# A new order and a new choice of engines for the same 4,836 steps of a one-core layer kernel

## Chip, core and metric

The kernel runs on one core of a Trainium2 chip. Its time is the device time of one execution in microseconds, the median of several runs. A core has five engines with a queue each, worked off in order: TensorE (PE; its weight loads are listed as PEld), VectorE (DVE), ScalarE (ACT), GpSimd (POOL), and SyncE (SP), which here issues the transfers. An instruction at the head of a queue that waits for another engine holds up everything behind it.

## What is computed

One layer of a decoder trunk on 512 tokens of width 1024, in float32: a normalised and modulated input goes into one projection whose columns feed a recurrent head group (convolution, RG-LRU scan) and an attention group (compressed, selected and windowed keys), then an output projection, a residual, and an MLP with a squared ReLU.

```python
for l in range(DEPTH):
    mod = jax.nn.silu(c) @ ada_w[l] + ada_b[l]
    sh1, sc1, g1, sh2, sc2, g2 = jnp.split(mod, 6, axis=-1)
    h = modulate(rms_norm(x, pre_norm_mix[l]), sh1, sc1)
    y = hybrid_mixer(h, w_in[l], ...)     # z = h @ w_in; rnn and att from its columns; concat @ w_out
    x = x + (1.0 + g1[:, None, :]) * rms_norm(y, post_norm_mix[l])
    h = modulate(rms_norm(x, pre_norm_mlp[l]), sh2, sc2)
    y = jnp.square(jax.nn.relu(h @ w_ff1[l])) @ w_ff2[l]
    x = x + (1.0 + g2[:, None, :]) * rms_norm(y, post_norm_mlp[l])
```

## The kernel before

Every float32 matmul is done in three: a weight tile `raw_w` is split into `hi_w` (a rounded copy, often on ScalarE) and `lo_w` (the difference, on VectorE or GpSimd), the activations likewise into `h` and `h2l` or `lo`, and TensorE adds the three products (`mm3`, L948). The sequence is four blocks of 128 tokens.

The program is written as streams, generators that record steps instead of issuing them (`Clocks.record`, L295). The order of work along the time axis is: the opening up to about 20 us (streams XL, WM, XN, SU, TR, MW), the projections of `h` (PR, with AW and the compressed keys; until about 160 us), the recurrent group's vector work (VW: scan over `r`, gates `g0` to `g3`, whose projection result in the PSUM bank `f` is copied to `r` by ScalarE), attention scores (AS: matmul `s<-K,Q`; `p<-s,tab` on VectorE; the exponential `p<-p,mx` on ScalarE; the scaling `p<-p,den` on any of three engines), attention values (AV: transposes `tp<-ident,p`, their copies `pt<-tp`, matmul `pv<-pt,V`), the output projection (CO, FA: `f<-hi_o,h`; weights `raw_o`), the residual and second norm (RS), its transposes (TH: `h`, `h2l`), the up projection (UF for its first two slices, `pv<-h,hi_f`; then UP, `f<-h,hi_f`), the first down pass (DA, with sums of weight blocks `raw_A..` and of activations `fs`), and the second down pass (DN, from 525 us) with the last norm and the stores. Beside all of them run the modulation sums (AD: `ar<-ar,silb`, `accT`), the loads (WL) and the splits of weights (WS).

Two tables fix what happens on the chip. `PLACE` (L69) has, for each stream, one letter for each step that can run on more than one engine: a (ScalarE), d (VectorE), p (GpSimd); `Clocks.put` (L305) reads it. `PLAN` (L90) lists all 4,836 steps, two characters each, and `Clocks.flush` issues them in that order. So the order in each engine's queue is the order of its steps in `PLAN`, the transfers on SyncE's queue among them:

```python
text = "".join(PLAN)
for a, b in zip(text[::2], text[1::2]):
    (way,) = self.nodes[ALPHA.index(a) * len(ALPHA) + ALPHA.index(b)].ways
    way[2]()
...
mine = PLACE.get(self.name, "")[k:k + 1] if PLACE is not None else "adp"
ways = [w for w in ways if w[0][0] in (usual if mine in ("", ".") else mine)]
```

Matmuls are at L396, transposes at L400, ScalarE's operations at L407, VectorE's and GpSimd's at L441, stores at L483.

Of the kernel before, what the change touches and what calls it, by code (L numbers as in the profile page):

```python
# [15 lines left out]
P = 128  # L16
S = 512
D = 1024
# [77 lines left out]
    '2d372E2K2~2G3S2c2j2g2e2f382b2l2i333V3T2k39352r2h2n342/2m2q363W2*2p3X2%2o2-3*3!3U2,3x3#2<2]3c3Y2?2=3y3C3Z'
    '3I3$2:3a2{2@583d2^3O3F3D3z3b3%3e3h3&3J3n3+3P3(3L3i3o3,3R3)3t4#3k3/4H3?3u4%3:3q4F3{3@45463w3A473G3M484M2.'
    '3|3f4O494C3l3r4A3<4N4B3-4g3=4G4$4h4i4k4l4m4j4Q4^4&4n4P4+4o4,4-4]GY4(4.2+2>4~4S5L504)2;514*3]5K4/2[4_3~4{'
    '4d2_3^5Y3E413K3Q52425D3B5X5M4|4}59533H3j445E5h5A5B5C435F5H5G3N5g5J3p3v5O3g3m5I5N5S3;5$3[5P3s4b7%5T3.5R3>'
    '4a3_3}4J5Q5#5Z5U5V5a5b5i5j5k4I5-5W5l5m5d5n5o5p5q5,5r4X5s7&4V5t5u4K5e627)6;4c6-5v4L5w6<6.6/5x6=5y615z5f6d'  # L100
    '5!5%6>6e4W6f7>6N674U6_6M5c6:7(68696@6A7?6V6B6{6?6C4e4R6D5_6E5&4Z4T6g6F4Y6G6H6I6U5(5)6[6J6|7+6K4f6q6}6L7|'
    '6h6O5*6p6P6i5+6]6^816Q6~6R6j6y5.5/6S6x6T6W5:726k5{716l6X6m6n5;5<7a6Y5=5>6a5?7b5@5[6Z5]73706o7c5^5}5|6r5~'
    '6c607C636s7B646t7R6u656v6w6b667N746z6!7S7D6#6$6%8L7z757T6&7@7!766(7[7o7]7}6)7~80777*7#788279836*847A7s85'
    '7t7p6+7q86877M88897r8A8B7w7u8V8W7vGW8Z8C8D8X7x7E8b7^8K8d937F8Y947,8E7-977_7.GZ957G997H7y7I9&7/8e4E7J8j9('
    '7K8k9)7L9+7O8h8F9,7P8f6,8G8O8i9E8P8QGa987Q7U9A9F7V8R9I7W9K7X9J9G7Y8M8S7Z8g7$7d8T7:7e8c9:7fG@9H8^8_9L8{9;'
# [1704 lines left out]
```

## Time and profile before

| | |
|---|---|
| median of 3 runs | 627.62 us (626.68 to 628.64) |
| the profiled execution's own time | 627.82 us |
| its span, first to last instruction | 626.0 us |
| PE, DVE, ACT, POOL busy | 95%, 86%, 55%, 33% of the span |
| PE instructions, weight loads not counted | 3060 |
| mean granted clock of TensorE | 0.991 of full speed |

The profile is of one execution. PE counts as busy from the start of a matmul to its modelled end, so that back-to-back matmuls overlap a little and short gaps between them don't show.

### The profile page before, as it was taken

What the parts mean: (1) busy time and instruction counts of PE and PEld (TensorE: products, weight loads), DVE (VectorE), ACT (ScalarE), POOL (GpSimd) and SP (SyncE); (2) the same over time, 40 slices, a digit from 0 to 9 for tenths busy, and PEclk for the clock granted to TensorE, in tenths of its full rate; (3) what the DMA queues carried; (4) which work ended last, traced back from release to release, by engine and by line L of the source; (5) the groups of instructions that cost most, each with busy time, mean ns of one, the idle gap of its engine ahead of it and who ended that gap; (6) DMA issues with size and microseconds to landing.
All of it is one profiled execution on the core that took longest, in us unless ns stands there. A gap on an engine that the chain in (4) does not pass through costs nothing.

```text
span 626.0 us, 9043 instructions
## 1 busy us (share of the span) xinstructions
PE 596.3 (95%) x3060; PEld 497.9 (80%) x3060; DVE 539.2 (86%) x1072; ACT 346.1 (55%) x696; POOL 209.1 (33%) x209
## 2 busy tenths in 40 slices
PE   7999999998999999989999999999999999999992
PEld 6888788966777898869887888888887888878881
DVE  5986988979999988988888968787688789999897
ACT  6654525698999999687251220322322247465563
POOL 5001301652663175453204547641351231000113
PEclk9999999999999999999999999999999999999997
DMA  8968895430503302015664334254544426756613
GB/s 351 416 250 318 320 299 191 131 136 1 202 2 129 141 2 102 1 35 176 229 222 168 115 133 137 101 169 157 180 135 147 155 69 204 238 179 202 198 56 134
DMA packets 29430, 102.15 MB, mean 163 GB/s; under 512 B 3268, under 2 KB 3524, under 8 KB 29384
## 3 DMA queue, kind: packets, MB, share of 16 engines
q1 hardware_dynamic: 29240, 101.50, 46.4%
q8 instruction: 24, 0.39, 0.3%
q14 instruction: 22, 0.18, 0.1%
q10 hardware_dynamic: 144, 0.07, 0.0%
HBM read 99.47 MB, written 2.10 MB: 162 GB/s over the span
## 4 chain that ended last, share of the span: by engine, by line
PE 73%; DVE 11%; DMA 6%; ACT 5%; issue 3%; DVEq 0%; SPq 0%; ACTq 0%
PE f L396 36%; PE s L396 14%; PE pv L396 13%; PE tp L396 7%; DMA ar<-in_ada_t 4%; PE tp L400 4%; DVE r L441 3%; ACT p L407 2%; DVE fT L441 2%; ACT r L407 2%; DVE ar L441 1%; DMA raw_A11l<-in_wd 1%; DMA raw_A10l<-in_wd 1%; DVE p L441 1%; DMA r<-in_x 1%
## 5 line engine op out<-in xcount | busy, mean ns | idle before, releaser
L396 PE MATMUL f<-h,hi_f 128*128 128x512 f32 x224 | 87.7, 392 | 0.0
L396 PE MATMUL f<-h,lo_f 128*128 128x512 f32 x224 | 87.2, 389 | 0.0
L396 PE MATMUL f<-h2l,hi_f 128*128 128x512 f32 x224 | 87.2, 389 | 0.0
L407 ACT ACTIVATE fT<-f 128x512 f32<-128x512 f32 x30 | 17.8, 594 | 71.2 <-PE f L396 71.2
L396 PEld LDWEIGHTS f<-h,hi_f 128*128 128x128 f32 x224 | 42.1, 188 | 8.8 <-issue 0.2
L396 PEld LDWEIGHTS f<-h2l,hi_f 128*128 128x128 f32 x224 | 42.0, 188 | 8.6
L396 PEld LDWEIGHTS f<-h,lo_f 128*128 128x128 f32 x224 | 42.0, 188 | 8.5
L396 PE MATMUL f<-hi_o,h 128*128 128x512 f32 x128 | 47.7, 414 | 0.0
L407 ACT ACTIVATE p<-p,mx 128x32 f32<-128x32 f32 (+4 forms) x96 | 45.1, 472 | 3.8 <-DVE mx L441 3.6
L441 DVE TENSOR_TENSOR lo_f<-raw_f,hi_f 128x1024 fp32r<-128x1024 f32 x29 | 40.1, 1383 | 6.9 <-ACT hi_f L407 6.6
L400 PE MATMUL tp<-ident,p 128*128 128x128 f32 x192 | 41.6, 273 | 1.9 <-DVE pt L441 0.9
L396 PE MATMUL pv<-pt,V 128*128 128x256 f32 x160 | 42.2, 316 | 1.1 <-ACT pt L407 0.7
L441 POOL TENSOR_SCALAR p<-p,den 128x32 f32<-128x32 f32 (+4 forms) x43 | 35.7, 863 | 18.5 <-DVE den L441 15.5
L396 PE MATMUL s<-K,Q 128*128 128x288 f32 (+4 forms) x128 | 38.4, 336 | 0.5 <-DVE Q L441 0.3
L441 DVE TENSOR_TENSOR pt<-tp,pt 128x512 fp32r<-128x512 f32 (+1 forms) x56 | 33.6, 609 | 3.3 <-ACT pt L407 1.9
L407 ACT ACTIVATE hi_f<-raw_f 128x1024 fp32r<-128x1024 f32 x24 | 24.9, 1056 | 18.7 <-PE f L396 13.0
L396 PEld LDWEIGHTS pv<-pt,V 128*128 128x128 f32 x160 | 27.8, 189 | 6.1 <-DVE pt L441 2.1
L396 PE MATMUL s<-r,fs 128*128 128x512 f32 x96 | 32.5, 389 | 0.0
L396 PE MATMUL pv<-r,fs 128*128 128x512 f32 x96 | 31.8, 391 | 0.4 <-DVE r L441 0.4
L400 PEld LDWEIGHTS tp<-ident,p 128*128 128x128 f32 x192 | 25.0, 140 | 7.8 <-issue 1.8
L396 PE MATMUL tp<-r,fs 128*128 128x512 f32 x96 | 30.6, 389 | 0.0
L441 DVE CUSTOM_DVE_ANT_0 ar<-ar,silb 128x1024 f32<-128x1024 f32 x16 | 21.6, 1352 | 6.4 <-DMA ar<-in_ada_t 6.4
(732 smaller groups left out, 1817.0 us busy)
## 6 DMA issues: line engine op xcount, KB each, us to landing
raw_f<-in_wf SPq DMA_DIRECT2D x32, 512.0 KB, 3.5
p<-in_ada_a SPq DMA_DIRECT2D x16, 512.0 KB, 8.0
ar<-in_ada_t SPq DMA_DIRECT2D x16, 512.0 KB, 4.4
ar<-in_ada_r SPq DMA_DIRECT2D x16, 512.0 KB, 4.0
r<-in_x SPq DMA_DIRECT2D x8, 512.0 KB, 4.6
raw_c<-in_wc SPq DMA_DIRECT2D x8, 512.0 KB, 5.2
raw_o<-in_wo SPq DMA_DIRECT2D x8, 512.0 KB, 6.4
raw_a<-in_wa SPq DMA_DIRECT2D x8, 384.0 KB, 7.5
```

Source lines behind the costliest of these rows:

```text
L396: lambda: self.nc.tensor.matmul(out, lhs, rhs, start=start, stop=stop))
L400: self.issue("pe", 0.109, [out], [src], lambda: self.nc.tensor.transpose(out, src, ident))
L407: return "act", cost, lambda: self.nc.scalar.activation(out, src, func, scale=scale, bias=bias, **kw), func
L441: return eng, cost, lambda: fn(out, *args, **kw), None
```

## The change

Nothing but `PLACE` and `PLAN` differs: the same 4,836 steps with the same operands. 259 steps get another engine (69 each in WS and DA, 59 in AS, 12 in AV, 10 in AW, 9 in TH, 8 in DN, 7 in UP, 6 in VW, 5 in FA, 4 in XN, 1 outside any stream). TensorE has 2,922 steps before and after and 207 transfers are issued; ScalarE goes from 568 to 573 steps, VectorE stays at 938, GpSimd from 201 to 196. TensorE's order changes from its second instruction until the first down pass, most steps by fewer than 60 places; the second down pass keeps its order on TensorE. On SyncE's queue the first 33 loads are the same; after them neighbours are exchanged, by 1 to 12 places.

```diff
 PLACE = {
-    'AS': 'papaaaadapadapdppadpddpdpapddapadppdpppapapppdaadddddaapdpdaadpdpapadddppaaappppdappppppapppapap'
-        'appapadppdppaadd',
-    'AV': 'dadaadddddaddddaaddadaaaaaaaaadaaaadaaaadaaaadaaaadaaaad',
-    'AW': 'adadaaddpppddpdp',
+    'AS': 'paaaappddaaadapddppdppappddpdaaadpadpppadppppppddppdaaaddadappadppappppaapaaapadpddpppppddpdapap'
+        'pppapadapddpaaaa',
+    'AV': 'aaaaddadddaadddadddddaaaaaaaaaaadaaaaaaadaaaaaaadadaaaad',
+    'AW': 'aaaaaaaadpdpddpd',
...
-    'FA': 'dddppdpdpddp',
+    'FA': 'pppppppddddp',
     'RS': 'ppadddddadda',
-    'TH': 'daddaadpddddaadddddddappddpddadd',
+    'TH': 'ddddaapdadddaadddddpaadpddddaadd',
...
-    'VW': 'pppdddpddppdppppppp',
+    'VW': 'dpddppppdppdppppppd',
...
-    'XN': 'aaaaaadaaaaa',
+    'XN': 'aaaddddaaapa',
 }
 PLAN = (
-    '000O0P020Q0106400R0S0T0U0V0M074p4q084r0a0W0y040b4sGX4t090c030&0d0X0A554u0C4v054w0e4x0(0-4y0Y0H0N4z4!0D4:'
...
+    'q_p{p|p}qJq5qIq6q7q3q8p;q9qAqfqBqCqDq4qEqFqGqLqhqMqgqNqOqPqQqXqiqRqSqTqUqVqYqWqZqcqdqKqeqjqlqmqaqnqqqoqr'
...
```

Decoded, this is the order of four stretches (step's output<-input; a stretch of one engine's queue):

```
ScalarE, projections' end
  before: sigmoid r | exp r x4 | sqrt r x2 | Q<-f x2 | r<-f (g0) | sqrt r x2
  after:  sigmoid r | exp r | r<-f (g0) | exp r x3 | sqrt r x3 | Q<-f x2 | sqrt r
VectorE, start of the MLP
  before: h2l_1 | h2l_0 | h2l_2 | h | r<-f | h | lo_f0 | r<-r,h x2 | h2l_5 | h2l_4
  after:  h2l_0 | h2l_1 | h2l_3 | r<-f | lo_f0 | h2l_4 | h | r<-r,h x2 | h2l_6 | h2l_5
          (h2l_3 comes from GpSimd, h2l_2 goes to it; one h of ScalarE's nine transposed copies ahead of
           hi_f0 goes to VectorE, one h of VectorE to ScalarE, behind hi_f0)
GpSimd, opening of the projections
  before: lo_x0 | r<-r,vecs | r<-r,vecs
  after:  lo_x0 (both r<-r,vecs are on VectorE)
GpSimd, tail
  before: ar<-ar,fT | ar<-ar,fT | fT15<-ar,g2row1
  after:  ar<-ar,fT | fT15<-ar,g2row1 (the second ar<-ar,fT is on VectorE, stat<-stat ahead of where it was)
```

## Rows read from the trace of the kernel before

**Rows 1.** The page, part 1: the span, and of each engine its busy time, share of the span and instructions.

```profile
span 626.0 us, 9043 instructions
...
PE 596.3 (95%) x3060; PEld 497.9 (80%) x3060; DVE 539.2 (86%) x1072; ACT 346.1 (55%) x696; POOL 209.1 (33%) x209
```

**Rows 2.** The view of windows, by stage (from:to and length in us, then the busy us of each engine in it with its instructions, the granted clock of TensorE as a part of full speed, the DMA share and rate).

```profile
0.00:100.00 100.00, 92.21 (x524) 79.07 (x525) 81.96 (x163) 52.28 (x84) 15.71 (x28) 1.00 0.85 319
100.00:145.00 45.00, 44.66 (x257) 36.14 (x258) 38.57 (x126) 37.47 (x105) 20.11 (x18) 1.00 0.38 129
145.00:200.00 55.00, 49.09 (x261) 39.03 (x259) 53.31 (x157) 52.28 (x135) 30.14 (x31) 1.00 0.21 78
200.00:262.00 62.00, 62.00 (x402) 54.34 (x401) 56.68 (x166) 54.55 (x134) 28.14 (x38) 1.00 0.22 77
262.00:300.00 38.00, 35.22 (x234) 31.83 (x233) 33.23 (x53) 28.34 (x48) 16.02 (x21) 0.96 0.32 103
...
526.00:626.00 100.00, 87.51 (x384) 71.66 (x383) 91.89 (x129) 53.37 (x82) 14.31 (x9) 0.96 0.51 170
```

**Rows 3.** The view of waits of TensorE over the whole span: which matmul (its output) waited for which engine's instruction, us in total, number of waits, the longest.

```profile
PE f L396 <- ACT r L407: 2.9, 2, 1.9
PE pv L396 <- DVE lo_f L441: 1.4, 1, 1.4
PE pv L396 <- ACT hi_f L407: 1.1, 1, 1.1
PE tp L400 <- DVE pt L441: 0.9, 1, 0.9
PE s L396 <- POOL r L441: 0.8, 1, 0.8
PE f L396 <- DVE Q L441: 0.8, 1, 0.8
PE pv L396 <- ACT pt L407: 0.7, 1, 0.7
PE s L396 <- DMA raw_c<-in_wc: 0.7, 1, 0.7
...
PE f L396 <- DVE fs L441: 0.5, 1, 0.5
```

**Rows 4.** The timeline of ScalarE from 139 to 149 us: start, duration, what it does (xN: N of a kind in a row), and in brackets the idle time before it with its releaser.

```profile
140.53 2.57 ACT L407 ACTIVATE r<-r,sp 128x512 f32<-128x512 f32 x4
143.11 1.28 ACT L407 ACT_TABLE_LOAD   x1
...
145.72 1.20 ACT L407 ACTIVATE Q<-f 64x512 fp32r<-64x512 f32 x2 [0.15 <-PE f L396]
146.94 0.60 ACT L407 ACTIVATE r<-f 128x512 f32<-128x512 f32 x1
```

**Rows 5.** The timeline of TensorE at the same place, the same columns.

```profile
145.28 0.40 PE L396 MATMUL f<-h,lo_q 128*128 128x512 f32 x1
147.59 0.50 PE L396 MATMUL f<-h,hi_g 128*128 128x512 f32 x1 [1.91 <-ACT r L407]
```

**Rows 6.** The timeline of VectorE from 270 to 284 us, where the MLP begins.

```profile
273.69 1.64 DVE L441 TENSOR_TENSOR h2l<-h,h 128x256 fp32r<-128x256 f32 x3
...
276.36 0.53 DVE L441 TENSOR_SCALAR h<-tp,a,s 128x256 f32<-128x256 f32 x1
276.81 1.21 DVE L441 TENSOR_TENSOR lo_f<-raw_f,hi_f 128x1024 fp32r<-128x1024 f32 x1
```

**Rows 7.** The view of windows around the first MLP matmuls, the columns of rows 2.

```profile
276.00:280.10 4.10, 2.35 (x15) 1.91 (x16) 3.89 (x7) 3.57 (x7) 2.26 (x3) 1.00 0.25 78
280.10:283.50 3.40, 3.40 (x17) 3.40 (x18) 2.83 (x4) 3.28 (x4) 0.48 (x1) 0.50 0.15 60
```

**Rows 8.** The timeline of VectorE and then of GpSimd from 67.5 to 74.5 us.

```profile
68.41 3.32 DVE L441 CUSTOM_DVE_ANT_0 ar<-ar,silb 128x1024 f32<-128x1024 f32 x1 [0.60 <-DMA ar<-in_ada_t]
...
68.27 2.37 POOL L441 TENSOR_TENSOR lo_x<-raw_x,hi_x 128x1024 fp32r<-128x1024 f32 x1 [17.91 <-ACT hi_x L407]
```

**Rows 9.** The timelines of the tail, 609.5 to 626 us: VectorE, then GpSimd.

```profile
611.04 1.32 DVE L441 TENSOR_TENSOR stat<-stat 128x1 f32<-128x1 f32 x2
...
610.71 1.57 POOL L441 TENSOR_TENSOR ar<-ar,fT 128x512 f32<-128x512 f32 x1 [0.83 <-ACT fT L407]
613.51 1.55 POOL L441 TENSOR_TENSOR ar<-ar,fT 128x512 f32<-128x512 f32 x1 [1.24 <-ACT fT L407]
```

**Rows 10.** Groups of instructions between 145 and 262 us, one shape each (line, engine, operation, output<-input, shapes and count, then busy us and mean ns of one, then idle time before): GpSimd, ScalarE, VectorE.

```profile
L441 POOL TENSOR_SCALAR p<-p,den 128x384 f32<-128x384 f32 x3 | 3.9, 1316 | 1.4 <-DVE den L441 1.4
...
L407 ACT ACTIVATE p<-p,den 128x384 f32<-128x384 f32 x7 | 4.1, 606 | 0.3 <-ACT p L407 0.3
...
L441 DVE SCALAR_TENSOR_TENSOR accT<-ar,sil,accT 128x512 f32<-128x512 f32 x8 | 6.0, 745 | 0.0
...
L441 DVE TENSOR_TENSOR_SCAN r<-p,r 128x512 f32<-128x512 f32 x4 | 5.9, 1476 | 0.0
L441 DVE SCALAR_TENSOR_TENSOR lo_o<-raw_o,vecs,hi_o 128x512 fp32r<-128x512 f32 x8 | 5.8, 740 | 0.0
...
L441 DVE TENSOR_TENSOR lo_o<-raw_o,hi_o 128x1024 fp32r<-128x1024 f32 x3 | 3.8, 1260 | 0.0
...
L441 DVE TENSOR_SCALAR p<-p,den 128x384 f32<-128x384 f32 x6 | 2.7, 476 | 0.0
```

More of the change, by code (lines that the diff above doesn't have):

```diff
@@ L96 @@
[L96 to L105, printed above, removed]
@@ new lines @@
+    '0o1E0p1k0q15141F171v1G0[19161B180r1A1D1H1l0s1w1I0t1M0u1J0v1N0w1=0x1Q1W0$1V1m1U1K1n1o1>1b1p1x1q0<1r1c1@1T'
+    '1]1L1R1s1Z1S1?2L1[1t1Y1^1_1{1a1|1X1e552Q1u1z1}1i1h2M1%201f1d1g0]2x541$211+1y2X1#1;1~221&2&1-2O2N1,2s232P'
+    '1<2y1!2R28052E2t2z2S2T292V1*1:2F2Y2U1)1(272K2W2Z1.262v302u2(2a2D2w1/2g56252}2)242!312f2#322A2|332B2$2C2H'
+    '2G372m2~2c2%2I2i383V2J2l3c2b2e3S392r2o352/2?2,343T2{2d2j2*2h362p2:2k3y2-2@2=2n3W2^3U3d3D2<2]3!3x2q3e2.3*'
+    '3J3C3#3I3z3X4G3+3Y3O3Z3A3P3F3a3,3L3$3%4#3R3(3k3b4%3i3h4H3&3q2>3G3n3)3t3/3?573{3M463o3u3:453@3|482+4M2;47'
@@ new lines @@
+    '3f4N3w3l4B3<4O3r3-4C4$4g494h4i4A2_4j4]3E4^4k2[4&4l4Q4m5L4n4R4(4F3=4o3^4T4+424,4P4-3K414.GX3]4~434S4)4*3B'
+    '5K4/50514_4{3H4|5X5Y4}3Q523N535D44595h5E3j5M3~5A5B5N3g5S5F3p3v5C5O5H5g5G5P5J3;3m5Q5Z5$5a5I3[5R3s5b5V3.5i'
+    '5j5#3>5k5l5m3_5T5n5-4J5o5p4d5q5r5W3}4I5U5s5t5d5u5v5,7%5w5x4U6d7&4b6e4L5e626;7(6-7)5c6.4K5y5z6<5!6=6/6:4c'
+    '67616>4V5%68694W6@6_7>6N5&4X6f0N5f6{4a4Y5(6[6A6M6B5)5*5+5.4Z6g6V6C6D6?587?6E6]6|6U6h6}6F6^6G6H4f5_6q6I6i'
+    '6~7+6J7|725/6j6p736k5:6l6K5{5;6y5<6L5=765>5|6x6O745?6P6Q6m716R6S6T6W6X5@7a6Y5[6n756Z5]7b5^6a6o5}6r6c7c5~'
@@ new lines @@
+    '6sGY60777063646t7R6u6v6b7C656w667o7S6z6!6#6$7z6%7p7B78797@7[7A7D6&7T7!7]7}6(7~7N807q7r6)7E7w7s7M8283848V'
+    '858W7t7u8X8ZGW7v8b866*877x7,7^8d887F817G8e897#7H7-8A936+7I7.7J8j7_8B8C8f8h7K8k4e948D7L7O977P954E8K7Q7/8E'
+    '8Y8F8G7U8c8O999EGZGa7V8P7y8Q9F7W7*8R9&987X8S7Y8g7Z9KG@7d8T7:967e7f9A7$7g7h7;8i8^8_8L7i9G8a9I8{7<9(7j8U8|'
+    '7=8}8l6,8~9:9L9;8u909H8m8v9+8w8s8r8x917k929J9B8y9<8t8z8q8!8#7l8$9=8%8&9C8(8H8n8)G]8*9D8+9V9W9)8,9M8o8-7m'
+    '8.9,9lAUAO8/9N8p8:8I9r9R8;8<9U8=8>9m9X8?9sAP9S9Y8J9Z8@9n9t9o9aG[AQ8[9b9OAVAS9v9Q7{9c9w9uAR9xAp9p9P9yAW9z'
@@ new lines @@
+    '9!9#9*8]9$8M9q9%AX9d9eA59f7nAv9gAqAE9h9-9TAFB.Aw8N9.G^9/9>AGA69?ArA79iG_9@B/9[AtAH9]9j9^AIAxA8CbCcATCdAJ'
+    'A.C99_A/9{CiA9CjAYAuAKA>CAALCkAMCpA?AyCqAACrAZCBABC#AaA<AcC$C%A:Ab9|A;A@9}9~C+A=AdAeBDHPBEAzA0BLAgCNC,AN'
+    'AfA!A#ACAhADA(AiAjBFAsC-BJCOA$BHA[C/A%A)BtBKA1A&BIC:BMA2BGB1B5A*C;A3BuBRAkA]B2BPC<9kBNAlC=B6B3A+BvA,A^B4'
+    'B,A~BwA-A|A_B7C1A}AmHQB-BhA4BiA{HRHbC_C2C>B:B9C3B0CWHSCPCXCHB8C4BjBACIBkCQBnBBCJCVAoCRBlCUBCCLAnCKBmBoBp'
+    'CMBxCSBcC{C|CZC~CTBqByC@BrD0C[C]DVBdD1BzC^B#D2ChD3CaB!D4BsDWD6CYD7DPD8CeD9DQB$CuDAB%DBDCB(CmDDDXDEDFCoDG'
@@ new lines @@
+    'DHCvDICfDJCwDKB&CnDRDSDLCzB)DTDMDUC)DYB*CtDZDOC!B+DaDeDbDND$BeClC*DuFhDcDdC&DhD@D[CxD]DiD^C?BODjD_B;DvD%'
+    'D{DkD!C(D&D|DwDyD}BSBfDlBgDmD#D+DnCsCyBQB<DoDpDxDqBTD)DzCgD~BUC}DrD*DsE6D,E0E1D(E7DtBaE2D-BVBZBbD.EsC.BX'
+    'EtBYEuEvBWEwD=B@FjB|D5ExECB[E*B]E3B^E+EAD<B}EDE,B=DfE[B_E]E^B~E_E{EBB>FlE4E8EEEaEbB{E|EgFAFnEeEhEQFBE9Ei'
+    'E5EGEFEcFCC0D?FIEjD>FJHEFKFdEdFeD/F%HFC5E-FfE=EfE.EHEIE/FgE;C6EkC7D:C8F|E>ElB?EJD;FLErEWFkEKE?EmELEpFRF&'
+    'CCEREXFMEqESEMFPFSG1ENFoCDEYH>HNETFNEOFTF,EZEnEPEUEoF~G,F}F<CEG0FiF4F5F=HKF6EVF7FmF-EyG-F.CGEzE}G3E!CFE#'
@@ new lines @@
+    'E$F:E~HLG4E%L)F0F1F>GUF_F2GxHeGrF8GsL*G.F3E&FpHJE<F9FtGVG6FuFqH?L(E)FvGyE(FrDgFwGvG/FsF(GtG:F{FOFzF!H4FD'
+    'H5FxH@E@F#H[FGGzF$G;G2G8H6F)FyHAFHHBE:H]G5FQH8HGH^HCHHFUH_H{F*H#HDG9FVG7F@HpGuH$FWHOGAF[HqF+FZGNH%GBHIFa'
+    'GCHrGOHtIUH9H:IFGPH7GHGIFbGJGKFcGDIGGLH&GQH|H}GRHsGMGlGSGmHuGnGTGoGhFYGiG!GjH;H(GpGbGcGkFXFEH<GdGeGqH~H='
+    'FFI0GfGwHZF?GgIYHcG<I1IVH)G{G=IZF]IHF;HdIWH*G|IaIJG>HMI?F/HaJSL&IXI!I#I)HYG#I*IKI&I@G?G$H0I+G}JTG)H1GEI$'
+    'JUG~JVI(HfH2I[IIH3JWG*G(JHHgJLJXI%HTJ.GFG%HhHjHiJ/I,JMHkG+HvG&HlGGH/JNHmI6HwJOHnHUHxJPHVI7JII-HoI2H+JBHy'
@@ new lines @@
+    'J:HXHzJ;JQI.J<I;H!JRI9I3I4I5IAMlHWILJCH-I8IMIBICIQI/J=IDJFJ?J@JDJ>JJJ[H.IRIPJ]H,JzJ^J_MnIbJtINKOKPISIEIO'
+    'MvKQJuIfIcKHJEIgKqI>J!JvKrITI:IdI=MwI<JxKIJKIoIeIhIpIqIrIiMmK8IsIjIkIuJwIvIwItKsJyKtIxMoKuIlKvIyKwJ#KJMs'
+    'MtI|K9IzKxI]JGI^MuI_I}I~J$J7KCJ0KAI{KDJ1J3J%J4J5KGJ8KKKEKiJ2KjKFJ6JYKmJ9KkKyJhJiJ&KzKnJAJ-JZK/KoJaKBJbK:'
+    'JjJcInJkJ*JnK[K=JlLSLTK;J+KpK]JoJmLULhJpK<J,LCLDKlImJdK^K0JqJ{LELiJrK1J|LjJeLGJsLpLHK_J}LqLtLKKWKXLFJfKY'
+    'K{KLK2J~KMLIK3LuLJK4K|J(K5JgKcK}KNK6KZLrLvL0LwKaL1K7KdM0L2LsLxKeKbKRL!M1KSL3LyL#KTK>KfL$J)M4KgM5K!K#KUK&'
@@ new lines @@
+    'L%K$M2M6KhK(K%McM3MdM7K)LVK+LzLWK,K*LXK-LYMeMgLbLZK.LcL7KVLdM8LeK?LaMhL8M:LfL+K@M9MAL,MiL/L9MkMEL4L:MfLg'
+    'L;L-L.L<M>LAL=L5LBL?L@L^F^LkM?L>L_L{L|L[LnM@L]M;L}MQL6MRLLK~OrL~LMLoMSMTLNMDM<MFMUMVMYMZOpMWNCNDNHLOMXMj'
+    'MHNEMaOqM*MLM+M,NIM-MbNGMCM$M.OtMOM%LPM[MIMGNsMPM/LQOuOxN2MyNJN3NtMzLRN6N4NuM]OvNKN7NwN8OsM^N5MpMBO@M&Oy'
+    'MqOwM=N^NxMxM_MrN!M{M~MMNyN0N_M|N}N{O[N9NFN~M}NANaN1NLOMNzONNTNBOzNbNeNfNgO0O]NvNcNdNhNoM(O^NMNiM)NUNSNk'
+    'NlNRNmNjNpNVNWNPO_O!NnO{NNNXNQNqN#O#N-LlN$OQMNO|NYNrN|N.N%NZO}N/O~N:NON=P0N>N;ORLmN&N?N(N@N)N<PVN[O2OSPi'
@@ new lines @@
+    'OON*M!PjN]MJO6P1O3O7O8OTO4O5OCOGO9OHOPODOAP4PWOUOIOEPXOFOBPkO1OdOJPYP2N,MKOeOKPlOVPZOWP5OfOZOgOLOhOiPmOl'
+    'OaOjPnO*OmOYOkPoObOnN+P3PpPqOcO+OoO:P6O,O-PaO.O;PrO$O%PbO/O&O<O=PcO>PdOXO)PsPBPtO?PFPCPDPGPuPEPHPIPPPLPJ'
+    'PeO(PMPfP7PQPKPgPNPRPSPhPOP(P,PTP)P8P*Q2P9PvQ3PUQ4P-M#P+Q5P.P:PAP;P<PwP/P=P>PxPyP?QPQQQ6PzQRP@P[P]QSP^QT'
+    'Q7P!P_QVQ8P{QUQ9QAP|P#QXQBQWQCQDP}QYQEP~Q0P$QZQ1P%Q[Q]Q^QaP&QdQFQ_QxQ{QbQeQnQcQfQgQIQoQ|QhQpR8QJQiQqR9RA'
+    'QrQGRBQkQyQHQsRCQjRDQtQKQ)Q*QuQ+Q,QzQ-Q!Q#Q.Q$REQvQ%QLQ&Q}QlQ(Q=QmQ~Q>QwRPQ?QMR0Q@QNQ/RRRQR1RSRFQ;R2RTRU'
@@ new lines @@
+    'RvQ:RGRwRxR3RyRHRzRJR!R#R4R$R%R&RIR(R5R)R*RVR6Q<R7R+SWR,RWR-R.R/R_R{R|R}QOR~RKS0RXS1S2S3SERYSFSGSHSISJSK'
+    'SLSMRLSNRZSOSPSQSRSSSTSURaSVSZRMSaSbScRNSdSeSfSgShSiROUGSjSkSlSmSnSXSoRlSpUHSqSrRbRcSsRdStUDSuSYReSvSwSx'
+    'SyRkRfRmUERnSzRoUJS!RgS#RqS$S%S&RhS(RpS)S*S+S,RrS-UIS.R:R;RsR<R=RtS/UNS:R>S;RiS<S=S4R?RjS5S6S7S>S?S8R@S@'
+    'RuS[S]S^S9R[S_S{S|S}SAR]S~T0T1R^SBT2T3T4SCT5T6T7SDT8T9UFTATBTCTDTETFU2TGTHUOTITJTKU3TLTMTNTOU1TPU5TQTRUP'
+    'U4TSUQTTTUTVTWTXTYUKTZTaURU6USUgTbULUhTcTdTeTfUMUUUiUjUkVEUlUaUmVFUnU7TgThVGVPTiUbUoTjUqTkU8UrUcTlTmTnUV'
```

143 lines of the change are left out of this document (52 added, 91 removed).

## Prediction

> **What bounds the kernel now.** I read the page's first part first. TensorE is busy 95% of the span, VectorE 86%, ScalarE 55%, GpSimd 33% [rows 1]. The same 2,922 TensorE steps run after the change, at the same sizes, so the time can only come out of TensorE's idle time, out of its clock, or out of the ends. TensorE's idle time is 626.0 - 596.3 = 29.7 us. The view of windows says where it lies [rows 2]: 7.8 us in the first 100 us (4.7 us of it is the wait for the first load), 0.3 from 100 to 145, 5.9 from 145 to 200, none from 200 to 262, 2.8 from 262 to 300, and 12.5 after 526, nearly all of it the tail behind the last matmul. Between 300 and 526 there is next to nothing to be had, whatever the order is. Then I read the view of waits, which gives these gaps their names [rows 3]. So the stakes are 3.1 us of the opening, 5.9 us of the attention stage, 2.8 us at the start of the MLP, 0.5 us in the second down pass and a tail that can hardly shrink: about 12.5 us, 2% of the time. A change that moves 259 steps and shuffles thousands can bring a per cent at most, and each wait that it makes new costs as much as one that it removes.
>
> The attention stage needs a second look. From 145 to 200 us VectorE is busy 53.3 of 55 us and ScalarE 52.3, while TensorE has 49.1 [rows 2]. TensorE waits there because two other engines are nearly full; if one wait goes, TensorE comes sooner to the next step that they have not done yet. So a gain in this stage is limited by what the two are relieved of, not by the sum of the named waits.
>
> **Part by part.** Durations are from the profiled execution: 627.82 us, of which 1.8 lie outside its span and stay; it stands 0.2 above the median of 627.62.
>
> *The gate projection.* TensorE stands still from 145.7 to 147.59 us, because the next gate block needs a PSUM bank that ScalarE has not copied out [rows 5]. ScalarE's copy (`r<-f`, 0.60) runs at 146.94, queued behind four exponentials (2.57), a table load (1.28), two square roots and two Q copies (1.20) [rows 4]. The new order puts it behind the first exponential, ahead of the other three. The Q copies at 145.72 stand between square roots and bring no table load of their own [rows 4], so a copy costs its 0.6 there too. But TensorE's order changes with it: the matmuls between the end of g0 and the first of g2 shrink from about 5.6 to 2.0 us (counted at 0.23 us for 512 columns, the distance of back-to-back starts), and in that time ScalarE has to finish an exponential (0.7) and the copy (0.6). That fits with some 0.5 us to spare. The wait of 1.9 goes; bounds -1.9 and 0. The second such wait (2.9 in two, so 1.0) keeps its cover of 1.3 us and stays [rows 3].
>
> *Attention's own waits.* Of the waits for `pt` and Q, three get more TensorE work ahead of them by my count of the tables: the transposes behind `pt` (0.9; cover 0.85 before, 1.2 after), the `pv` matmul behind ScalarE's `pt`, which moves to VectorE (0.7; 0.06 to 1.2), and the score matmul behind Q (0.3; 0.6 to 2.4) [rows 3]. A copy takes 0.6 to 0.7 us, so the last two go and the first halves: -1.4, bounds -1.9 and 0. Together with the gate this is 3.3. Against it stands the limit above: counted by its duration on its new engine, each moved step of this stage relieves ScalarE of 0.7 us and VectorE of 3.9 and loads GpSimd with 10.7. ScalarE has 55 - 52.3 = 2.7 us of slack and gets 0.7. I take -2.5 for the stage.
>
> *The start of the MLP.* The first up matmul waits 1.1 us for `hi_f0`, the second 1.4 for `lo_f0` [rows 3]. `lo_f0` stands on VectorE behind two `h` copies and three `h2l` that took 1.64 us together [rows 6]. In the new order one copy fewer is ahead of `hi_f0` on ScalarE (0.45 sooner) and two `h` copies fewer are ahead of `lo_f0`. Then `lo_f0` starts behind `hi_f0` at 275.6 instead of 276.81. That gives at most 1.2; I take -0.9, as the normalised `r` that feeds all of this is not earlier on VectorE's queue. Bounds -2.5 and 0.
>
> *The clock.* After this stage, in which TensorE is busy 2.35 of 4.1 us, the granted clock is 0.50 for 3.4 us, the lower of its two levels (1.2 GHz), though TensorE is busy all the time [rows 7]. At half speed that is 1.7 us lost. The waits before it get shorter but don't vanish, and I leave the dip where it is: 0, bounds -1.7 and +1.7 (a second dip elsewhere).
>
> *The opening.* A wait of 0.8 for GpSimd's `r` is for a step that goes to VectorE, with 0.5 us more TensorE work ahead of it: -0.5. A wait of 0.8 for Q is that of a VectorE step behind `ar<-ar,silb`, which took 3.32 us at 68.41 while GpSimd worked on `lo_x0` from 68.27 [rows 8]; the two `r` steps behind `lo_x0` leave GpSimd but `lo_x0` stays, and the cover falls from 6.5 to 5.2: -0.4. The `raw_c` load that was awaited (0.7) is issued earlier: -0.3. Bounds for the three -2.3 and 0. Three copies that go from ScalarE to VectorE ahead of the first projection matmuls: +0.2, nothing to +0.7.
>
> *The first down pass and the second.* 50 steps change between VectorE and GpSimd in DA, and 400:526 has no idle TensorE to give or take; cover there is above 5 us for nearly all, so 0. The wait of 0.5 for `fs` falls away, as the GpSimd step beside which its predecessor was slow moves to VectorE: -0.5, bounds -0.5 and 0.
>
> *The tail.* VectorE's two `stat` adds at 611.04 take 1.32 us for 128x1 operands, and end just as GpSimd's add of 610.71 does, at 612.3 [rows 9]; in the new order the first is issued ahead of that. The add of 613.51 goes from GpSimd (1.55) to VectorE, 0.60 us in a row that has no gap. Worked through by hand the last store starts 0.35 us earlier: -0.35, bounds -0.5 and +0.9.
>
> *New waits.* The trace can't show them. The dependencies with under 1.6 us of TensorE work ahead number about as many after as before (attention's transposes 48 then 54, `pv` 41 then 36, scores 62 then 50, opening 7 then 13). Selecting the waits of before and seeing them relieved says little alone: others, tight now, were lucky in this execution. Bounds: none, or as many as eight of the usual size, 0.7 [rows 3], 5.6. I take three: +2.1.
>
> Sum: -2.5 - 0.9 + 0 - 1.2 + 0.2 - 0.5 - 0.35 + 2.1 = -3.15, so 627.8 - 3.15 = 624.7, and 0.2 lower against the median: **624.5 us**.
>
> **Rivals.** *Waits only change places.* The same count of tight dependencies gives the same waits elsewhere; TensorE stays at its 12.5 us of gaps less the 0.85 of tail and `fs`, and the opening pays 0.2: 627.0. For it speaks that the counts hardly move, against it that ScalarE's copy had been plainly late. That the new tables fail to do what they say is not open, as each queue follows `PLAN`; that their order is good only in a replay comes to this same case.
>
> *Slower: GpSimd blocks VectorE between 145 and 200 us.* A scaling of 128x384 takes 1.32 us on GpSimd against 0.61 on ScalarE and 0.48 on VectorE [rows 10], and while GpSimd works, a VectorE instruction with its operands in SBUF is held until GpSimd is done: 3.32 us, 1.32 for two small ones [rows 8, 9]. Such VectorE work (`accT`, the scan, both `lo_o`) is 6.0 + 5.9 + 5.8 + 3.8 = 21.5 us of the 110 that VectorE works from 145 to 262 [rows 2, 10], a fifth. 10.7 us more on GpSimd would give back 2.1 of VectorE's 3.9; and each scaling on the way to a transpose with too little cover costs 0.7 to 0.85. 24 steps of AS go to GpSimd and 25 leave it, but in this stretch the large ones come. It decides from the point where more than five of them have under 1.3 us of cover: six at 0.75 with the 2.1 cost 6.6 against my 3.15 gained: 631.1. For it speaks the fuller VectorE, against it that the stage's VectorE load still ends lower.
>
> The Trainium skill says this outright ("Perfetto Trace Analysis", Optimizing Scalar/DVE Operations): GpSimd and VectorE share a read port, so moving operations between them might not help; and "SBUF — State Buffer" (SBUF: two separate sides) has it as a lock held for a whole instruction, the loser fully blocked, for VectorE operations with two SBUF inputs among others. The 1.32 us of two 128x1 adds agree with a lock. By that rule alone the stage gains nothing and the case is this rival's.
>
> *Faster still.* The MLP's first waits shrink so far that the clock stays up (-1.7), and one new wait comes instead of three (-1.4): 621.4.
>
> **How the numbers follow.** Forecast 0.45, waits that change places 0.25, slower 0.18, faster still 0.12. About 0.3% (1.9 us) is what a measurement of this kernel tells from no change. Of the forecast's case nine tenths lie below 625.7; of the second a tenth below it, three quarters within the bound and 0.15 above; of the slower one nine tenths above 629.5. Faster 0.41 + 0.12 + 0.02 = 0.55, same 0.04 + 0.19 + 0.02 = 0.25, slower 0.04 + 0.16 = 0.20. The range reaches from below the fastest case by another 2.4 (the opening's bound) to near the slower case: 619 to 630.5; it leaves out half of the slower case and little below.
>
> **What would show it.** Right: no wait above 0.5 us for ScalarE's `r` near 147; `lo_f0` starting within 0.2 us of the end of `hi_f0`; TensorE's idle time from 145 to 200 at 3 to 4 us instead of 5.9; the tail's first `stat` add not ending with GpSimd's add; three or so new waits of 0.4 to 0.9 in the opening and in attention. Wrong: VectorE's busy time from 145 to 200 not lower, with scans and `lo_o` above 2 us beside GpSimd (the slower case); named waits of TensorE again near 12 us in sum (waits that change places); a granted clock of 0.5 at another place, or none at 280.

## The result, and the profile after

The changed kernel takes 624.51 us (median of 8 runs, 622.05 to 626.37); the kernel before 627.19 (median of 8). The ratio on record is 0.9932, with a 95% interval from 0.991 to 0.9955: 0.7% faster, or 4.3 us (2.8 to 5.6). It isn't the quotient of the two medians, which differ by 2.7 us only; so the gain is known to a few us, no better. The profiled execution took 622.05 us, 620.2 of them its span, which is the fastest of the eight; the two profiles differ by 5.8 us. What follows is read with that in mind. Of the experiments' executions three slow ones (636, 857 and 2,100 us) are left out of the ratios.

The first part of the page and the view of windows by stage, to be held against [rows 1] and [rows 2]:

```profile
span 620.2 us, 9034 instructions
...
PE 594.4 (96%) x3060; PEld 496.3 (80%) x3060; DVE 541.4 (87%) x1072; ACT 343.8 (55%) x701; POOL 194.8 (31%) x204
```

```profile
145.00:200.00 55.00, 51.50 (x282) 41.70 (x280) 53.33 (x155) 52.29 (x136) 39.96 (x40) 1.00 0.33 116
...
262.00:300.00 38.00, 35.64 (x240) 31.50 (x239) 34.14 (x55) 27.53 (x48) 11.37 (x18) 1.00 0.33 111
```

TensorE's idle time in the attention stage is 55 - 51.5 = 3.5 us, where it was 5.9. VectorE and ScalarE are as full as before (53.33 and 52.29), GpSimd has 9.8 us more. From 262 to 300 us TensorE is idle for 2.4 us (2.8 before). The view of waits of TensorE, against [rows 3]:

```profile
PE s L396 <- DVE ident L441: 5.5, 1, 5.5
PE f L396 <- ACT r L407: 1.7, 2, 1.2
PE f L396 <- DVE Q L441: 1.1, 1, 1.1
PE s L396 <- DMA raw_c<-in_wc: 0.9, 1, 0.9
PE pv L396 <- DVE lo_f L441: 0.8, 1, 0.8
PE pv L396 <- DVE h2l L441: 0.7, 1, 0.7
PE s L396 <- DVE Q L441: 0.6, 2, 0.3
...
PE pv L396 <- ACT hi_f L407: 0.4, 1, 0.4
...
PE tp L400 <- DVE pt L441: 0.4, 1, 0.4
```

The wait of 1.9 us for ScalarE's `r` near 147 us is gone; of the two that remain one (1.2) is for the copy that comes next on ScalarE (155.80), which was there before (1.0). The waits for `pt` are down to 0.4 or out of the list. Larger than before are those for `h2l` (0.7 after 0.3), for Q in the opening (1.1 after 0.8) and for Q ahead of the scores (0.6 in two after 0.3 in one). The first wait, for `ident`, holds TensorE's start until 5.5 us; it was the load of `r`, until 4.7. ScalarE's timeline shows the step that was moved, against [rows 4]:

```profile
139.08 0.72 ACT L407 ACTIVATE r<-r,sp 128x512 f32<-128x512 f32 x1
139.71 0.58 ACT L407 ACTIVATE r<-f 128x512 f32<-128x512 f32 x1
140.19 1.94 ACT L407 ACTIVATE r<-r,sp 128x512 f32<-128x512 f32 x3
```

The copy of the first gate block runs at 139.71, between the exponentials, 7 us sooner than before. At the MLP's start (ScalarE, then VectorE, against [rows 6]):

```profile
271.00 1.05 ACT L407 ACTIVATE junk<-r 128x1024 bf16<-128x1024 f32 x1
...
272.04 1.05 ACT L407 ACTIVATE hi_f<-raw_f 128x1024 fp32r<-128x1024 f32 x1
...
272.63 0.75 DVE L441 SCALAR_TENSOR_TENSOR r<-f,stat,r 128x512 f32<-128x512 f32 x1 [0.50 <-PE f L396]
273.30 1.22 DVE L441 TENSOR_TENSOR lo_f<-raw_f,hi_f 128x1024 fp32r<-128x1024 f32 x1
...
275.22 1.28 DVE L441 TENSOR_TENSOR r<-r,h 128x512 f32<-128x512 f32 x2
```

`lo_f0` starts 0.2 us after `hi_f0` ends, at 273.30. TensorE waits 0.4 and 0.8 us for the two, not 1.1 and 1.4. But two sums `r<-r,h` (275.22) stand ahead of `h2l_5`, for which it waits 0.7. The granted clock stays at 1.00 here, against [rows 7]:

```profile
273.00:277.00 4.00, 2.54 (x17) 2.14 (x17) 4.00 (x8) 4.00 (x9) 0.80 (x3) 1.00 0.31 117
277.00:280.00 3.00, 2.75 (x20) 2.55 (x21) 2.85 (x4) 3.00 (x4) 0.00 (x0) 1.00 0.20 41
```

And in the tail (VectorE, then GpSimd, against [rows 9]) the small add no longer meets GpSimd's:

```profile
605.93 0.15 DVE L441 TENSOR_TENSOR stat<-stat 128x1 f32<-128x1 f32 x1
...
607.07 1.30 POOL L441 TENSOR_TENSOR ar<-ar,fT 128x512 f32<-128x512 f32 x1 [2.44 <-ACT fT L407]
```

### The profile page after: what moved, and what is told of

Same layout as the page of the kernel before. It is cut to its first block, busy times and chain, and to the rows that moved or that the text cites. A ratio compares the mean times of both kernels' runs of the same rounds, so it can differ in the third digit from the quotient of the medians.

```text
span 620.2 us, 9034 instructions
## 1 busy us (share of the span) xinstructions
PE 594.4 (96%) x3060; PEld 496.3 (80%) x3060; DVE 541.4 (87%) x1072; ACT 343.8 (55%) x701; POOL 194.8 (31%) x204
## 4 chain that ended last, share of the span: by engine, by line
PE 82%; DVE 9%; DMA 4%; ACT 3%; issue 1%; DVEq 0%; POOL 0%; ACTq 0%
PE f L396 42%; PE s L396 15%; PE pv L396 12%; PE tp L396 8%; PE tp L400 4%; DMA ar<-in_ada_t 3%; DVE r L441 2%; DVE p L441 1%; DVE fT L441 1%; ACT p L407 1%; DVE ar L441 1%; DVE pt L441 1%; DMA raw_B0l<-in_wd 1%; ACT r L407 1%; DMA vecs<-in_vecs 1%
## 5 line engine op out<-in xcount | busy, mean ns | idle before, releaser
L441 POOL TENSOR_SCALAR p<-p,den 128x32 f32<-128x32 f32 (+4 forms) x39 | 39.1, 1013 | 17.8 <-DVE den L441 14.0
L396 PE MATMUL tp<-r,fs 128*128 128x512 f32 x96 | 32.2, 389 | 0.0
L396 PE MATMUL s<-r,fs 128*128 128x512 f32 x96 | 31.2, 389 | 0.0
L441 POOL TENSOR_TENSOR ft<-fT 128x256 f32<-128x256 f32 x13 | 13.8, 1068 | 54.1 <-DVE fT L441 33.1
L396 PEld LDWEIGHTS s<-K,Q 128*128 128x128 f32 x128 | 23.0, 189 | 5.8 <-DVE mx L441 1.2
```

The source lines that it names most:

```text
L396: lambda: self.nc.tensor.matmul(out, lhs, rhs, start=start, stop=stop))
L441: return eng, cost, lambda: fn(out, *args, **kw), None
```

## The experiments

Each ran on one chip beside the kernel before (median 628.2 to 628.3 there), and its ratio is against that. The us beside a ratio are worked out from it. Most are hybrids of the two tables: of "before until, new until, before" the first and last steps come in the order and on the engines of before, those between in the new ones. Where I give TensorE's lead or lag at a time, it is how much earlier or later the same amount of matmul work is done, from the starts of all matmuls in two profiles.

**The stretch from 99 to 261 us alone.**

```diff
-order: before
+order: before until 99 us | new until 261 us | before      (86 steps on another engine)
```

> The kernel before until about 99 us, the new order and engines from there until about 261 us (end of projections, recurrent work, attention), and the order and engines of before again from the output projection's end on. My theory (the named waits of the attention stage are what the change removes): 3 to 3.5 us faster than before, about 624, with the wait for ScalarE's copy of the first gate block near 147 us gone. The rival that the gain comes from the MLP's start and the clock: within 1 us of before. The rival that waits only change places: within 1 us of before, with new waits in this stretch that sum to what went.

Measured: ratio 0.9977 (0.9957 to 0.9996), so 1.5 us faster (0.3 to 2.7), less than I expected. The wait at 147 us is gone in the profile; TensorE's lead over before is 3.2 us at about 200 us and 2.0 to 2.1 from 245 us on: a third is given back in the second half of attention.

**The stretch from 261 us to the end alone.**

```diff
-order: before
+order: before until 261 us | new      (155 steps on another engine)
```

> The kernel before until about 261 us, the new order and engines from there to the end (residual, transposes, MLP, tail). My theory: the first two up matmuls wait 1 us less, the tail is half a us shorter: 1 to 1.5 us faster, about 626; if the drop of the granted clock at 280 us falls away as well, as in the changed kernel's profile, 1.7 us more, about 624.5. The rival that attention carries the whole gain: within 0.5 us of before.

Measured: 0.9943 (0.9924 to 0.9963), 3.6 us faster (2.3 to 4.8): more than half of the gain is here. The rival that attention carries all falls. The two halves together give 5.1 us where the whole change gives 4.3; with their intervals that is the same, and it leaves nothing that the opening would have to add.

**Order alone, engines alone.**

```diff
 e3:  order new, engines of before
 e4:  order of before, engines new
```

> The new order for all steps, with the engines of before. My theory (the order of the copies and splits in their queues is what counts, the choice of engine in a few places only): 1.5 to 3 us faster than before, about 625. The rival that the choice of engines carries the gain: no faster than before, 627 or more.

> The order of before for all steps, with the new engines. My theory: within 2 us of before, rather slower (up to 629), since the 259 steps come into queues whose order was not made for them, and the copy of the first gate block stays late (its wait of 1.9 us stays). The rival that the choice of engines carries the gain: 624.5.

Measured: 1.0204 (1.018 to 1.0228) and 1.0349 (1.0302 to 1.0396), slower by 13 and 22 us. Both expectations of mine fall, and the rival's too: an order is made for one choice of engines. Neither half of the change has a gain of its own, and such halves can't be used to divide one.

**The copy of the first gate block alone.**

```diff
 ScalarE's queue
-sigmoid r | exp r x4 | sqrt r x2 | Q<-f x2 | r<-f (g0) | sqrt r x2
+sigmoid r | exp r | r<-f (g0) | exp r x3 | sqrt r x2 | Q<-f x2 | sqrt r x2
```

> The kernel before with one step moved: ScalarE's copy of the first gate block (r<-f, g0) goes ahead of the exponentials 2 to 4 instead of behind the exponentials, two square roots and two Q copies. My theory with its limit (VectorE and ScalarE nearly full in this stage): the wait of 1.9 us at 147.6 is gone in the profile, and TensorE at 200 us is 0.7 to 1.5 us ahead of before, not 1.9; time 626.5 to 627.5 where before has 628. If there is no such limit: 1.9 us ahead at 200 us. The rival that waits only change places: less than 0.3 us ahead at 200 us.

Measured: 1.0008 (0.9983 to 1.0033), no gain. TensorE's timeline:

```profile
145.48 0.40 PE L396 MATMUL f<-h,hi_g 128*128 128x512 f32 x1
...
149.06 0.54 PE L396 MATMUL s<-K,Q 128*128 128x288 f32 x2 [3.07 <-DVE Q L441]
```

The next gate block's first matmul (145.48) starts without a wait, and then TensorE stands for 3.1 us ahead of the score matmul, for Q. The wait changed its place and lost nothing; at 200 us TensorE is 0.2 us behind before. My expectation was wrong: the new order also puts TensorE's other gate matmuls ahead of those scores, and without them the early copy is worth nothing. Whether it is worth something with them is the next run's question.

**133 to 150 us alone, and 152 to 261 us alone.**

```diff
 e11: before until 133 us | new until 150 us | before      (135 steps, 6 on another engine)
 e12: before until 152 us | new until 261 us | before      (1129 steps, 54 on another engine)
```

> The kernel before, but for the new order and engines from about 133 to 150 us (135 steps: the copy of the first gate block early, and TensorE's matmuls of the next gate block ahead of the score matmuls). My theory after the run with the copy alone, whose wait moved on to the score matmul behind Q: both parts are needed, the two waits of 2.1 and 0.5 us become 0.4 and 0.6, and TensorE is 1 to 1.6 us ahead of before at 150 us; at 200 us still 1 or more if VectorE and ScalarE don't limit the stage, 0 to 0.7 if they do. The rival that waits only change places: 0 at 150 us.

> The kernel before until about 152 us, the new order and engines to about 261 us, and before again. The wait of 2.1 us at 147 us stays. My theory: the waits behind pt between 172 and 193 us get shorter, and TensorE gains 1 to 1.5 us between 152 and 262 us, the rest of what the new order gave from 99 to 261 us (2.7 us in the profile). If the gate carries that gain alone: 0 to 0.3 us.

Measured: 1.0014 (0.9987 to 1.0041) and 1.0009 (0.9987 to 1.0031). In the profiled execution of e11 TensorE ran at under a third of its usual pace from start to end (the span is 2,098 us; why is not known), so its waits can't be read; its time shows no gain above 0.8 us. So the early copy with TensorE's new order beside it has no gain of its own that is clear of noise either. In e12's profile TensorE gains 2.3 us on before from 152 to about 212 us and has lost 1.4 of it again by 245. So more than half of what the new order wins there is given back before attention ends. That the two stretches alone show no gain in time and e1, with both and the stretch from 99 us, 1.5 us, is open: the two intervals allow 0.8 us each, and the seams of the hybrids may have a price of their own.

**The MLP's start alone, and what follows alone.**

```diff
 e6:  before until 261 us | new until 300 us | before      (390 steps, 11 on another engine)
 e9:  before until 300 us | new                            (2142 steps, 144 on another engine)
```

> The kernel before until about 261 us, the new order and engines to about 300 us (second norm's transposes, first two slices of the up projection), and before again. My theory: the first up matmuls' waits fall from 1.1 + 1.4 to 0.4 + 0.8 us, with a new one of 0.7 for h2l; 0.5 to 1 us, and if the granted clock stays up, 1.7 more: 1 to 2.5 us faster, 626 where before has 628. The rival that the MLP's half of the gain comes from the down passes and the tail: within 0.5 us of before.

> The kernel before until about 300 us, the new order and engines from there (up projection, both down passes, tail). My theory: the waits at the second down pass (0.3 to 0.8 and 0.7 us) shrink and the tail is 0.5 us shorter: 1 to 1.7 us faster, 626.6 where before has 628. The rival that this half carries the difference between the run with all of the MLP (0.57% faster) and the run with its start alone (0.14%): 2.7 us faster, 625.4. The rival that only the tail gains: 0.5 us.

Measured: e6 0.9986 (0.996 to 1.0012), 0.9 us faster within -2.5 and +0.8; in its profile the waits are those of the changed kernel, and TensorE comes through the start 1.8 us faster than before. The clock stayed up in it, but that is worth less than the 1.7 us that the drop seems to cost. In the profile of e5, which has the order of before here, the clock stayed up too, and TensorE then waited for the next `lo_f`, which in the kernel before was ready when the slower TensorE came (before, then e5; the same matmul):

```profile
283.19 0.41 PE L396 MATMUL pv<-h,lo_f 128*128 128x256 f32 x1
283.25 0.39 PE L396 MATMUL pv<-h,lo_f 128*128 128x256 f32 x1 [0.76 <-DVE lo_f L441]
```

The three profiles with the order of before and no drop here (e1, e5, e12) come from 261 to 300 us 0.4 us faster than before. So of e6's 1.8 us the clock carries about 0.4 and the new order 1.4.

e9 measures 0.9953 (0.9929 to 0.9977), 3.0 us faster (1.4 to 4.5). So the half in which the profile of before showed almost nothing to gain carries most of it. What VectorE waits for between 440 and 526 us tells a part of why. Before:

```profile
DVE raw_A10l L441 <- DMA raw_A10l<-in_wd: 3.0, 1, 3.0
DVE raw_A11l L441 <- DMA raw_A11l<-in_wd: 2.4, 1, 2.4
DVE raw_A12l L441 <- DMA raw_A12l<-in_wd: 1.9, 1, 1.9
```

The MLP's start alone, which has the order of before in this stretch:

```profile
DVE raw_A10l L441 <- DMA raw_A10l<-in_wd: 2.6, 1, 2.6
DVE raw_A12l L441 <- DMA raw_A12l<-in_wd: 2.4, 1, 2.4
DVE raw_A11l L441 <- DMA raw_A11l<-in_wd: 2.3, 1, 2.3
DVE raw_A14l L441 <- DMA raw_A14l<-in_wd: 1.9, 1, 1.9
...
DVE raw_B0u L441 <- DMA raw_B0l<-in_wd: 1.3, 1, 1.3
```

The changed kernel, and e9:

```profile
DVE raw_B0u L441 <- DMA raw_B0l<-in_wd: 1.0, 1, 1.0
...
DVE raw_A13u L441 <- DMA raw_A13u<-in_wd: 0.2, 1, 0.2
```

```profile
DVE raw_B0u L441 <- DMA raw_B0l<-in_wd: 1.2, 1, 1.2
DVE raw_A9l L441 <- DMA raw_A9l<-in_wd: 1.2, 1, 1.2
```

In the order of before VectorE stands with a sum of weight blocks at the head of its queue until the load lands: 7.3 us in the three longest waits in the one profile, 10.5 in the five longest in the other. In the new order it is 1.2 and 2.4 us. TensorE doesn't show that as long as there is cover. Where `raw_A14l` comes later, it does; this is TensorE in e6's profile at the end of the first down pass:

```profile
521.22 0.39 PE L396 MATMUL s<-r,fs 128*128 128x512 f32 x1
523.29 0.73 PE L396 MATMUL s<-r,fs 128*128 128x512 f32 x2 [1.68 <-DVE r L441]
```

It waits 1.7 us for a sum `r` that stands on VectorE behind two sums of the block `raw_B0`. Besides e6 only e12 has this wait (0.5), and only these two of the six profiles with the order of before in this half (before, e1, e5, e6, e10, e12) show VectorE waiting over 0.5 us for `raw_A14l` (1.9 and 1.2). Over the six TensorE falls behind the pace of its matmuls by 1.7, 1.7, 1.7, 1.9, 2.6 and 4.5 us between about 480 and 610 us, over the five with the new one (the change, e2, e7, e8, e9) by 0.2, 0.6, 1.2, 1.3 and 1.4: 1.4 less in the mean. The tail from the last matmul to VectorE's last step is 9.11 us in all six and 8.59 in all five. Together that is 1.9 us, inside the interval of e9. Of the 1.4 us 1.3 have names: 0.6 in the mean is the wait for `fs` at 554 us (0.2 to 1.3 in the six, none in the five), 0.3 a wait for the sum of `raw_A11l` at 482 us, 0.4 that for the sum of `raw_A15l` at 523 us. Only the last two follow VectorE's waits for loads, with no gap on VectorE between (2.4 us until 477.0 in before, 1.9 and 1.3 until 509.5 and 521.3 in e6), so the loads account for about 0.7 us. What e9 gains beyond the 1.9 us is in no profile and stays open.

**GpSimd's extra steps.**

```diff
 changed kernel, engines of 12 attention score steps at 145 to 200 us
-GpSimd x12
+VectorE x6 (384 columns x3, 32 x1, den of 6 columns x2) | ScalarE x6
```

> The changed kernel, with the twelve steps of the attention scores that went to GpSimd between 145 and 200 us back on the engines that they had before (six on VectorE, six on ScalarE), in the new order. My theory (GpSimd's extra work is free, VectorE and ScalarE are nearly full): 0.5 to 3 us slower than the changed kernel, 625 to 627.5 where that has 624.5. The rival that GpSimd blocks VectorE: 1 to 3 us faster than the changed kernel, 622.

Measured: 0.9975 (0.9948 to 1.0002) against before, where the change has 0.9932: 2.7 us slower than the change (about 0.5 to 5 by the two intervals, which overlap a little), as my theory had it. The rival that GpSimd's steps are what costs falls as to its sign. But the reason is not mine either. GpSimd, VectorE and TensorE in turn:

```profile
183.88 2.37 POOL L441 TENSOR_TENSOR lo_o<-raw_o,hi_o 128x1024 fp32r<-128x1024 f32 x1
...
184.08 2.20 DVE L441 TENSOR_TENSOR den<-sm,eg 128x6 f32<-128x6 f32 x1
...
185.10 0.35 PE L396 MATMUL s<-K,Q 128*128 128x416 f32 x1
187.06 0.38 PE L396 MATMUL tp<-ones,r 128*128 128x1 f32 x2 [1.61 <-DVE stat L441]
```

VectorE's `den` is 6 columns wide, takes 0.16 us otherwise, and stands here for 2.20 us until GpSimd's `lo_o` is done; TensorE waits 1.6 us for the `stat` behind it, and then the clock falls:

```profile
188.00:192.00 4.00, 4.00 (x21) 3.73 (x21) 2.05 (x6) 4.00 (x15) 0.33 (x2) 0.61 0.01 2
```

In the changed kernel that `den` is on GpSimd, ahead of `lo_o`. So GpSimd does hold VectorE up, and this one of the twelve steps is well placed because it is out of its way; for the other eleven that is not shown.

**A repair.**

```diff
 changed kernel, five steps moved in their queues
 ScalarE:  +hi_f0 ahead of junk<-r;  +r<-f (the copy awaited at 156 us) ahead of one exponential (three instructions)
 VectorE:  +lo_f0 ahead of r<-f;  +h2l_5 ahead of r<-r,h x2
```

> The changed kernel with five steps moved in their own queues: ScalarE's hi_f0 ahead of the sum of squares of a residual tile, VectorE's lo_f0 ahead of the last residual product before it, h2l_5 ahead of two residual sums, and ScalarE's copy of the third gate block (1.0 us wait at 156 us) ahead of one exponential. My theory: the copy saves up to 1.2 us, the up projection starts 1 us sooner and its wait for h2l_5 (0.7) goes: 1.5 to 2.5 us faster than the changed kernel, 622.5 where that has 624.5. The rival that waits only change places (the residual chain, put back, makes later transposes wait): within 0.5 us of the changed kernel.

Measured: 0.9936 (0.9908 to 0.9964) against before, the same as the change. Its waits:

```profile
PE f L396 <- DVE Q L441: 1.6, 1, 1.6
PE s L396 <- DVE mx L441: 1.2, 2, 1.0
PE pv L396 <- DVE lo_f L441: 1.1, 2, 0.8
PE pv L396 <- DVE h2l L441: 1.0, 1, 1.0
...
PE tp L400 <- ACT p L407: 0.5, 1, 0.5
PE f L396 <- ACT r L407: 0.5, 1, 0.5
```

The wait for `r` is 0.5 (1.7 in two), that for `hi_f0` is gone. In their place stand 1.2 for score matmuls (`mx`, 0.5 in the change), 0.5 for a scaled `p`, 1.0 for another `h2l` and 0.8 for a second `lo_f`. Here the rival is right: where VectorE and ScalarE are full, five better places only move the waits.

**The opening alone.**

```diff
+order: new until 99 us | before      (18 steps on another engine)
```

> The new order and engines until about 99 us, then the kernel before. My theory: the wait for GpSimd's r at 49 us (1.0 us beyond the pace of the matmuls) goes, the start is 0.2 to 0.8 us later, the waits for raw_c and Q at 70 us stay: within 1 us of before. My prediction's term was -1.0.

Measured: 1.0094 (1.0063 to 1.0124), slower by 5.9 us. The profile shows it at the seam: until about 100 us TensorE is level with before within 0.3 us, then it waits 3.1 us for a score matmul (for `mx`, until 104.9), and the granted clock is 0.51 from 104 to 111 us. So this run says nothing against the new opening in its own kernel, only that TensorE's lead there is small.

## Why the prediction came out right, step by step

The forecast was a gain of 3.15 us; the measured one is 4.3 (2.8 to 5.6) by the ratio and 2.7 by the medians. That the sum came so near is in part luck: the gain of the opening was not there (about 1.0 too much), and that of the down passes was two thirds too small (about 2.1 too little).

- *The gate and attention, -2.5, with most of the +2.1 for new waits.* Alone it measures 1.5 us (0.3 to 2.7), inside what the two terms leave (2.5 to 0.4). The wait of 1.9 us went as the prediction said, and by the copy between the exponentials; e5 shows that the copy alone would have brought nothing, which I had not seen. That TensorE's new order beside it makes it pay is read from profiles (in e1's, TensorE's lead grows by 1.7 us between 140 and 152 us) and not shown in time, as e11 measures no gain. The `pt` waits shrank as forecast, that for Q ahead of the scores did not. The limit by two full engines fits: they stay at 53.3 and 52.3 us, and a third of the lead at 200 us is lost by 245. No run takes it apart.
- *The MLP's start, -0.9.* Waits of 0.4 and 0.8 us, `lo_f0` 0.2 us behind `hi_f0`, and one new wait of 0.7: right in place, and in size as far as e6's 0.9 goes, whose interval takes in zero; its profile would make it 1.4.
- *The clock, 0.* Right in the mean, wrong for the pair of profiles: the drop at 280 us is missing in the profile after, which the prediction had as a sign of being wrong. Three of the six profiles with the order of before at the MLP's start have the drop (before, e9, e10), none of the five with the new one (the change, e2, e6, e7, e8), so the shorter waits may well prevent it. But the price was mis-sized: the prediction put 1.7 us on it, and it costs about 0.4, since the next wait makes up for the rest. So it is a small part of the 5.8 us between the two profiles. Over the executions that were timed the mean clock is 0.990 after and 0.989 to 0.990 before.
- *The down passes and the tail, -0.85.* This is the step that failed, as a size: "between 300 and 526 there is next to nothing to be had". It measures 3.0 us (1.4 to 4.5). The tail is right (0.52, predicted 0.35) and the wait for `fs` is gone (0.6 in the mean of six profiles, predicted 0.5). What was missed are VectorE's sums that stand behind loads, about 0.7 us of TensorE's time in the mean. The profile of before is one execution in which they cost TensorE 0.4 us, but VectorE's own waits for the loads, 7.3 us, were in the trace; I read TensorE's waits only. About 1.1 of the 3.0 us has no name; the interval would allow that it isn't there.
- *The opening, -1.0 and +0.2.* Not there: the waits for `raw_c` (0.9) and Q (1.1) are longer in the profile after, not shorter. Only GpSimd's `r` (0.8) went, and the start is 0.8 us later. That is the order of VectorE's queue, and the prediction had not priced it: `sp`, which needs the load of `vecs`, now stands ahead of `ident`, which TensorE's first matmul needs. VectorE before, then after; last TensorE's wait before:

```profile
1.80 0.30 DVE L441 TENSOR_SCALAR ident<-p 128x128 f32<-128x128 f32 x1
...
4.79 0.17 DVE L441 TENSOR_SCALAR sp<-vecs 128x4 f32<-128x4 f32 x1 [4.79 <-DMA vecs<-in_vecs]
...
5.20 0.22 DVE L441 TENSOR_SCALAR ident<-p 128x128 f32<-128x128 f32 x1
...
PE s L396 <- DMA r<-in_x: 4.7, 1, 4.7
```

  The four profiles with the new opening (the change, e7, e8, e10) start at 5.4 or 5.5 us, those with the old one at 4.6 or 4.7. At about 100 us the four are between 0.8 us ahead of before and 0.7 behind. The six other profiles with the old opening are there between 2.0 ahead and 0.8 behind, and their wait for `raw_c` is 0.5 to 1.6 us. So a wait for a load varies from execution to execution by more than the term that I took for it, and a pair of profiles can't size the opening.
- *The slower rival.* VectorE's work with SBUF operands was drawn out by 3.5 us from 145 to 200 us, and by 3.4 before (each instruction against the usual time of its shape), although GpSimd works 9.8 us more. So the added steps found places where they hold little. Both signs that the prediction gave for this case were there, VectorE no less busy and a scan and a `lo_o` of 2.3 us, and the kernel was faster all the same; a scan of 2.3 us stood in before, too. The lock itself is real, as e7 shows: with fewer steps on GpSimd its VectorE is drawn out by 5.9 us in the same stretch. It was the place of the steps and not the amount of GpSimd's work that decided, and the prediction had priced the amount. The Trainium skill's sentence ("Perfetto Trace Analysis", Optimizing Scalar/DVE Operations) that moving work between the two might not help is not borne out here: e7, which moves twelve steps back, is slower than the change.
- *Waits that change places.* As a story for the whole change it falls (0.991 to 0.9955); TensorE's named waits behind its first one sum to 8.4 us in the profile after and to 12.4 in that of before. For single repairs it holds twice (e5, e8).

## What to carry to other kernels

Where helpers are nearly full, a long wait of the main engine rarely belongs to one step: move the step alone and the wait turns up one dependency on, so look at what TensorE could do in the meantime. Read the waits of the helper engines for loads as well as TensorE's own: a helper that stands at the head of its queue for a transfer is a loss that TensorE may show only in executions with late transfers (here in two profiles of six). Look what stands behind such a step as well: in the opening, `ident` behind one of them put TensorE's start back by 0.8 us in all four profiles. And put a number on how far two executions of one kernel differ before you divide a difference of two profiles into causes.
